# Feed-forward weight sums by adding transfers: turning the signs of a block scheme

## The chip, the core and the metric

The kernel runs on one core of a Trainium2 chip. Its five engines work in parallel and are tied by semaphores: TensorE (PE in the profile; PEld is its weight load), VectorE (DVE), ScalarE (ACT), GpSimd (POOL) and SyncE (SP). SP, and here also POOL, issue DMA transfers, which move data between the chip's main memory and the on-chip buffers. The metric is the device time in microseconds; the median of three runs is 1230.26 us (1228.70 to 1230.84).

## The reference, cut to what matters

Four decoder layers work on 256 tokens of width 1024. Layers 0 and 3 mix tokens with sparse attention (NSA), layer 1 with block attention (MoBA), layer 2 with a short gated convolution. After each mixer stands a dense feed-forward part with 2816 hidden columns:

```python
def swiglu(a, w_gate, w_up, w_down):
    return (jax.nn.silu(a @ w_gate) * (a @ w_up)) @ w_down

for i in range(DEPTH):
    a = rms_norm(h, norm_mix[i])
    h = h + mixer(a)                     # NSA, MoBA, convolution, NSA
    a = rms_norm(h, norm_ffn[i])
    h = h + swiglu(a, ffn_w_gate[i], ffn_w_up[i], ffn_w_down[i])
return rms_norm(h, norm_final)
```

Everything is float32. The change lies in `a @ w_gate` and `a @ w_up`.

## The kernel before

All weights stand in one array `w` of parts: a part is 128 x 1024 numbers (512 KB), eight tiles of 128 x 128, in the order in which PE uses them. A part is loaded by SP into one of six `raw` buffers (`load_part`), then split in two addends that the matrix engine multiplies: `whi`, a copy on ACT (L176), and `wlo`, the rest, a subtraction on DVE or, for a few named parts, on POOL (L180). Each product of float32 numbers is made of three matmuls: high by high, high by low, low by high. `whi` and `wlo` have five buffers each (`W_BUFS`), and `take` splits parts up to five ahead of their use (`AHEAD`), so ACT and DVE run ahead of PE until all five are full.

The feed-forward part (`ffn`) works through the hidden columns in groups of four tiles of gate and four of up: g = 0, 4, 8, 12, 16 and a last of two tiles. The groups 8 and 16 (`FAST_GROUPS`) go through `fast`: for the first four of the eight 128-row tiles of the inner dimension, tokens and weights are taken as 2 x 2 blocks, and seven block products take the place of eight. The weight blocks are B11, B12 (gate and up, first two tiles) and B21, B22 (gate and up, next two). Seven operands, in the order of `FAST`, are split into `shi` and `slo` (L136, L137) and multiplied (L442 to L444): B11, T1, B21, T2, B22, T4, T3. The T are sums and differences of blocks, which `combine` makes on DVE (L122):

```python
if what == "B11":
    b["T1"] = self.combine(b["B11"], b["B12"], b["B11"])   # B12 - B11
    b["T3"] = self.combine(b["B12"], b["B22"], b["B12"])   # B22 - B12
elif what == "T1":
    b["T2"] = self.combine(b["T1"], b["B22"], b["T1"])     # B22 - T1
elif what == "B21":
    b["T4"] = self.combine(b["B21"], b["B21"], b["T2"])    # B21 - T2
```

The four blocks are loaded by SP into four buffers of the tag `kx` (L132; `KX_BUFS`), which the `keys` of the two attention mixers also use. The sums on the token side are made by `token_sums` on POOL. The last four inner tiles of a fast group are ordinary parts, and their products (L476 to L478) are added to the same banks.

The hidden values are transposed on DVE, moved between partitions by 16 small transfers on SP (`move`, L411), and split into `ff` (`split`) at a set distance after the last move (`SPLIT_AFTER`, in half parts). `out_proj` multiplies them by the down weights (L226, L230).

Nobody writes the order of instructions on an engine out by hand: a scheduler takes the program in the order in which it is written, and puts each instruction on its engine's queue where its own estimate of times has its operands and buffers ready. On the chip each queue then runs strictly in that order: an instruction that waits holds everything behind it on its engine, and this holds for DMA issues on SP and POOL too. That is how loads of the feed-forward part's blocks come to stand amid the mixer ahead of it, where `kx` buffers come free of `keys`. POOL works in the attention mixers on the softmax scalings (L626) and on `wlo` of some output weights (L180).

Of the kernel before, what the change touches and what calls it, by code (L numbers as in the profile page):

```python
# [9 lines left out]
F32 = mybir.dt.float32  # L10
F32R = mybir.dt.float32r
AF = mybir.ActivationFunctionType
OP = mybir.AluOpType
# [10 lines left out]
DH = 64  # L24
# [9 lines left out]
MOVES = 4  # L34
SPLIT_AFTER = 4
FF_BUFS = 26
# [5 lines left out]
MOBA_ORDER = ("V k k q q k s V s T q q k s s P k T k q T P q P T P s q q T k s k T s s T P P T P P").split()  # L42
LO = {"nsa_out": "p", "moba_out": "vp", "A": "p", "F": "v"}
HI = {"moba_out": "v", "moba_q": "ava"}
# [4 lines left out]
FAST = ("B11", "T1", "B21", "T2", "B22", "T4", "T3")  # L49
FAST_GROUPS = (8, 16)  # L50
FFN_BANKS = ("BB BA", "AA AB", "BBAA", "AA BA", "BBAA", "B A")
KX_BUFS = 4
RUN = 2 * PART
LAG = 4
PROJ_BANKS = "AABB"
NSA_BY = ["p"] * 8
# [8 lines left out]
class Kernel:  # L65
    def __init__(self, ctx, tc, ap):
# [7 lines left out]
        self.raw = {}  # L74
        self.parts = {}
        self.jobs = []
        self.latest = []
# [42 lines left out]

    def combine(self, out, a, b):
        self.nc.vector.tensor_tensor(out=out, in0=a, in1=b, op=OP.subtract)  # L122
        return out

    def fast_part(self, x):

        q, what = self.seq[x]
        if what == "B11":
            self.blocks = {}
            for i, n in enumerate(("B11", "B12", "B22", "B21")):  # L130
                t = self.blocks[n] = self.block(n)
                self.load = self.nc.sync.dma_start(t, self.ap["w"][q + i])  # L132
        b = self.blocks
        hi = self.operands.tile([P, PART * P], F32R, tag="whi", name=f"shi{x}", bufs=W_BUFS)
        lo = self.operands.tile([P, PART * P], F32R, tag="wlo", name=f"slo{x}", bufs=W_BUFS)
        self.latest = [self.nc.scalar.copy(hi, b[what]),  # L136
                       self.nc.vector.tensor_tensor(out=lo, in0=b[what], in1=hi.bitcast(F32), op=OP.subtract)]  # L137
        self.parts[x] = (hi, lo)
        if what == "B11":
            b["T1"] = self.combine(b["B11"], b["B12"], b["B11"])  # L140
            b["T3"] = self.combine(b["B12"], b["B22"], b["B12"])
        elif what == "T1":
            b["T2"] = self.combine(b["T1"], b["B22"], b["T1"])
        elif what == "B21":
            b["T4"] = self.combine(b["B21"], b["B21"], b["T2"])

    def split_part(self, x):
        nc = self.nc
        q, what = self.seq[x]
        if what:  # L150
            self.fast_part(x)
            return
        lo_eng, hi_eng = (e.get(self.names[q], d) for e, d in ((LO, "v"), (HI, "a")))
        lo_eng, hi_eng = (e[q % len(e)] if q >= 4 else d for e, d in ((lo_eng, "v"), (hi_eng, "a")))
# [222 lines left out]
    def ffn(self, norm):  # L377
# [5 lines left out]
        q = P // 4  # L383
# [49 lines left out]
        def fast(tags):  # L433
# [45 lines left out]
            turned = self.sb([P, NT, 512], "pt", bufs=PT_BUFS)  # L479
            for t, (pg, eg), (pu, eu) in ((0, (gate0, p1), (up0, u2)), (1, (gate1, u3), (up1, p5))):  # L480
                nc.vector.scalar_tensor_tensor(eg, pg, r[t], eg, op0=OP.mult, op1=OP.add)
                nc.scalar.activation(eg, eg, AF.Silu)
                nc.vector.scalar_tensor_tensor(eu, pu, r[t], eu, op0=OP.mult, op1=OP.add)
                nc.vector.tensor_tensor(out=eu, in0=eu, in1=eg, op=OP.mult)
                nc.vector.transpose(turned[:, t], eu)
# [28 lines left out]
    def token_sums(self, norm):  # L514
# [7 lines left out]
        out = []  # L522
        for f, l, r, op in ((raw[0], a[1][0], a[1][1], OP.add), (raw[1], raw[0], a[0][0], OP.subtract),
                            (raw[2], a[0][0], a[1][0], OP.subtract), (raw[3], a[0][1], raw[1], OP.subtract)):
            nc.gpsimd.tensor_tensor(out=f, in0=l, in1=r, op=op)
# [210 lines left out]
    def nsa(self, j, norm):  # L736
# [12 lines left out]
        for a in range(2):  # L749
            nc.gpsimd.tensor_copy(xs[a][:, :, :, 16], pos[:, a, None, 8:].to_broadcast([P, 4, 8]))  # L750

        def put_raw(a, gp):
            def put(p):
                f = self.scaled(p)
                for i in range(2):
                    src = f[i * DH:(i + 1) * DH].rearrange("p (c r i) -> p i r c", i=2, r=8)
                    dst = xs[a][:, 2 * gp + i, :, :16]
                    nc.vector.tensor_copy(dst[:DH], src[:, 0])
                    nc.scalar.copy(dst[DH:], src[:, 1])
                if gp:  # L760
                    windows(a)
            return put

        def windows(a):
            for hf in range(2):
                for r in range(0, 8, 4):
                    x = self.ff([P, 2, S]).rearrange("p i s -> p (i s)").rearrange("p (r i g c) -> p r i g c", r=4, i=2, g=4)
                    src = xs[a][:, :, r:r + 4, hf:hf + 16].rearrange("p g r c -> p r g c")
                    nc.scalar.copy(x[:, :, 0], src)
                    nc.vector.tensor_tensor(out=x[:, :, 1], in0=src, in1=x[:, :, 0].bitcast(F32), op=OP.subtract)  # L770
                    if hf == 0:
# [494 lines left out]
```

## Time and profile before

| | |
|---|---|
| median of 3 runs | 1230.26 us |
| lowest, highest | 1228.70, 1230.84 us |
| profiled execution | 1231.72 us |
| its span, first to last instruction | 1229.9 us |
| granted TensorE clock, mean | 0.996 |
| PE, DVE, ACT, POOL busy | 98%, 80%, 60%, 23% of the span |
| moved by DMA | 231.40 MB, 213.33 MB of it read from main memory |

The profile is of one execution. A busy share is the sum of the instructions' durations; PE's matmuls overlap, so that 0.39 us stand for a matmul that starts 0.23 us after the one before it. "Idle before" is the time that an engine stood still ahead of a group of instructions, with the event that ended most of it. The feed-forward parts of the four layers run, by the chain of waits, from about 155 to 334, 451 to 629, 720 to 898 and 1044 to 1225 us; the mixers lie between.

### The profile page before, as it was taken

The numbers are of one execution on the slowest core, as the hardware profiler recorded it, in microseconds if no ns is written. First come the engines' busy times: TensorE is split into PE (matmuls) and PEld (weight loads), VectorE is DVE, ScalarE is ACT, GpSimd is POOL, SyncE is SP. The second block draws the span as 40 slices with busy tenths as digits, with TensorE's granted clock in tenths as the row PEclk, the third lists the DMA queues.
The fourth block names the chain that finished last, engine by engine and source line by source line (L and its number), as shares of the span: only waits on it lengthen the run. The fifth ranks groups of instructions, "written<-read, shape, count | busy, mean of one in ns | idle before, by whom it ended". The sixth has DMA issues, their size and how long they took to land.

```text
span 1229.9 us, 19380 instructions
## 1 busy us (share of the span) xinstructions
PE 1202.0 (98%) x6628; PEld 1043.2 (85%) x6628; DVE 985.2 (80%) x1743; ACT 732.5 (60%) x1300; POOL 288.0 (23%) x406
## 2 busy tenths in 40 slices
PE   7999999999999999999999999999999989999997
PEld 7988888888899888888888888888899878888886
DVE  7989788886778797887769797896759897889753
ACT  6789656564456535764444555574457896566543
POOL 1068640000111542000113260000230786400000
PEclk9899999999999999999999999999999999999999
DMA  8673265657654545666765655565647632655670
GB/s 313 221 235 88 85 225 165 211 183 252 193 172 154 167 136 175 240 202 194 278 197 164 191 183 175 200 237 164 244 155 244 207 115 74 208 177 198 200 266 35
DMA packets 96451, 231.40 MB, mean 188 GB/s; under 512 B 18272, under 2 KB 43232, under 8 KB 96352
## 3 DMA queue, kind: packets, MB, share of 16 engines
q1 hardware_dynamic: 95920, 229.61, 57.1%
q8 instruction: 52, 0.85, 0.3%
q10 hardware_dynamic: 432, 0.56, 0.1%
q14 instruction: 47, 0.39, 0.1%
HBM read 213.33 MB, written 1.05 MB: 174 GB/s over the span
## 4 chain that ended last, share of the span: by engine, by line
PE 83%; ACT 6%; DVE 5%; issue 2%; DMA 2%; POOL 1%; SPq 0%; POOLq 0%; ACTq 0%; DVEq 0%
PE psA L226 13%; PE psA L230 7%; PE psA L504 5%; PE psA L502 5%; PE psA L503 5%; PE psB L502 4%; PE psB L504 4%; PE psB L503 4%; ACT pr L622 3%; PE psA L208 2%; PE psA L206 2%; PE psA L207 2%; PE psB L226 2%; DVE wlo L180 2%; PE psB L444 1%
## 5 line engine op out<-in xcount | busy, mean ns | idle before, releaser
L176 ACT CAST whi<-raw 128x1024 fp32r<-128x1024 f32 (+1 forms) x363 | 373.3, 1039 | 289.6 <-DMA raw<-in_w 55.8
L180 DVE TENSOR_TENSOR wlo<-raw,whi 128x1024 fp32r<-128x1024 f32 (+1 forms) x350 | 428.3, 1241 | 130.1 <-ACT whi L176 106.4
L226 PE MATMUL psA<-ff,whi 128*128 128x512 f32 x686 | 181.8, 392 | 0.2 <-DVE row L1059 0.2
L226 PEld LDWEIGHTS psA<-ff,whi 128*128 128x128 f32 x686 | 124.8, 189 | 22.8 <-DVE row L1059 0.6
L626 POOL TENSOR_SCALAR pr<-pr,rc,gates 128x256 f32<-128x256 f32 (+1 forms) x128 | 76.9, 614 | 111.3 <-DVE rc L624 109.4
L206 PE MATMUL psA<-at,whi 128*128 128x256 f32 x352 | 101.3, 288 | 0.6 <-ACT whi L176 0.3
L208 PE MATMUL psA<-at,wlo 128*128 128x256 f32 x352 | 100.5, 286 | 1.1 <-DVE wlo L180 1.1
L230 PE MATMUL psA<-ff,wlo 128*128 128x256 f32 x686 | 101.0, 283 | 0.0
L230 PEld LDWEIGHTS psA<-ff,wlo 128*128 128x128 f32 x686 | 96.0, 191 | 5.3
L207 PE MATMUL psA<-at,whi 128*128 128x256 f32 x352 | 100.3, 285 | 0.0
L504 PE MATMUL psA<-whi,at 128*128 128x512 f32 x256 | 99.7, 389 | 0.0
L502 PE MATMUL psA<-whi,at 128*128 128x512 f32 x256 | 99.6, 389 | 0.0
L503 PE MATMUL psA<-wlo,at 128*128 128x512 f32 x256 | 99.6, 389 | 0.0
L136 ACT CAST shi<-B 128x1024 fp32r<-128x1024 f32 x56 | 58.9, 1051 | 54.2 <-DVE B L122 21.0
L293 POOL TENSOR_TENSOR ssq<-ssq,row 128x256 f32<-128x256 f32 x42 | 36.3, 864 | 207.9 <-ACT row L291 150.7
L180 POOL TENSOR_TENSOR wlo<-raw,whi 128x256 fp32r<-128x256 f32 x96 | 70.4, 767 | 34.7 <-issue 17.4
L137 DVE TENSOR_TENSOR slo<-B,shi 128x1024 fp32r<-128x1024 f32 x56 | 66.7, 1216 | 12.0 <-ACT shi L136 12.0
L502 PE MATMUL psB<-whi,at 128*128 128x512 f32 x192 | 75.2, 392 | 0.0
L504 PE MATMUL psB<-whi,at 128*128 128x512 f32 x192 | 74.8, 390 | 0.0
L503 PE MATMUL psB<-wlo,at 128*128 128x512 f32 x192 | 74.7, 389 | 0.0
L622 ACT ACTIVATE pr<-pr,mn 128x128 f32<-128x128 f32 (+1 forms) x160 | 71.2, 448 | 2.4 <-DVE mn L619 1.7
L206 PEld LDWEIGHTS psA<-at,whi 128*128 128x128 f32 x352 | 68.0, 193 | 1.9 <-DVE row L589 0.7
(293 smaller groups left out, 2688.4 us busy)
## 6 DMA issues: line engine op xcount, KB each, us to landing
raw<-in_w SPq DMA_DIRECT2D x368, 512.0 KB, 4.5
B<-in_w SPq DMA_DIRECT2D x32, 512.0 KB, 4.4
pt<-pt SPq DMA_DIRECT2D x320, 32.0 KB, 1.9
ff<-row SPq DMA_DIRECT2D x32, 64.0 KB, 3.4
keys<-keys SPq DMA_DIRECT2D x16, 128.0 KB, 2.9
h<-in_xt SPq DMA_DIRECT2D x4, 256.0 KB, 4.4
raw<-in_w SPq DMA_DIRECT2D x4, 256.0 KB, 4.7
pt<-pt SPq DMA_DIRECT2D x64, 16.0 KB, 3.1
```

The lines of the kernel that those rows point to most:

```text
L176: copy(hi[:, c], src[:, c])
L180: eng.tensor_tensor(out=lo[:, d], in0=src[:, d], in1=hi[:, d].bitcast(F32), op=OP.subtract)
L206: mm(out, wt[0], act[0], start=first, stop=False)
L207: mm(out, wt[0], act[1], start=False, stop=False)
L208: mm(out, wt[1], act[0], start=False, stop=last)
L226: mm(outs[o], w[0], acts[k].rearrange("p i s -> p (i s)"), start=(k == 0), stop=(k == n - 1))
L230: mm(outs[o][:, :S], w[1], acts[k][:, 0, :], start=False, stop=False)
L502: mm(o, a[:, 0, s], hi, start=(k == 0), stop=False)
L503: mm(o, a[:, 0, s], lo, start=False, stop=False)
L504: mm(o, a[:, 1, s], hi, start=False, stop=(k == KT - 1))
L622: nc.scalar.activation(pr[:, c], pr[:, c], AF.Exp, bias=mn[:, j:j + 1], scale=-1.0, accum_out=den[:, j:j + 1])
L626: {"p": nc.gpsimd, "v": nc.vector}[by[j % len(by)]].tensor_scalar(pr[:, c], pr[:, c], rc[:, j:j + 1], gates[j], op0=OP.mult, op1=OP.mult)
```

## The change

In place of four loads and four differences on DVE, a fast group now has:

- `start_sums`: SP loads B11 into a `kx` buffer t1 and B12 into t3; POOL then issues two transfers that add B12 to t1 and B22 to t3 as they write (`accum_op`). So T1 = B11 + B12 and T3 = B12 + B22. It is called up to 12 operands ahead of B11's split (`SUM_AHEAD`).
- B11 is loaded again, as an ordinary part, into a `raw` buffer; B21 and B22 are loaded into `kx` buffers when T1 is split. In all seven transfers of 512 KB a group where there were four: five by SP, two by POOL.
- T2 = T1 + B22 and T4 = T2 + B21 are still made on DVE, in place in t1.
- The signs of the token sums and of the last steps of `fast` are turned to match: subtractions for additions and the reverse, the same instructions on the same engines.
- `SPLIT_AFTER` goes from 4 to 6.

Three tables (`PAIRS`, `WINDOWS`, the entry `F` of `LO`) are new or longer, and name the same engine at each place as the code did before.

```diff
-SPLIT_AFTER = 4
+SPLIT_AFTER = 6
...
+SUM_AHEAD = 12
...
-    def combine(self, out, a, b):
-        self.nc.vector.tensor_tensor(out=out, in0=a, in1=b, op=OP.subtract)
-        return out
+    def start_sums(self, q):
+        nc, ap = self.nc, self.ap["w"]
+        self.blocks[q] = t1, t3 = [self.block(n) for n in ("T1", "T3")]
+        for t, i in ((t1, 0), (t3, 1)):
+            nc.sync.dma_start(t, ap[q + i])
+            nc.gpsimd.dma_start(t, ap[q + i + 1], accum_op=OP.add)
 
     def fast_part(self, x):
 
+        nc = self.nc
         q, what = self.seq[x]
-        if what == "B11":
-            self.blocks = {}
-            for i, n in enumerate(("B11", "B12", "B22", "B21")):
-                t = self.blocks[n] = self.block(n)
-                self.load = self.nc.sync.dma_start(t, self.ap["w"][q + i])
-        b = self.blocks
+        t1, t3 = self.blocks[q]
+        raw = {"B11": 0, "B22": 2, "B21": 3}
+
+        def load(name):
+            n = q + raw[name]
+            if n not in self.raw:
+                if name == "B11":
+                    self.load_part(n)
+                else:
+                    t = self.raw[n] = self.block(name)
+                    self.load = nc.sync.dma_start(t, self.ap["w"][n])
+            return self.raw[n]
+
+        if what == "T1":
+            load("B21")
+            load("B22")
+
+        def add(name):
+            nc.vector.tensor_tensor(out=t1, in0=t1, in1=load(name), op=OP.add)
+        if what == "T2":
+            add("B22")
+        elif what == "T4":
+            add("B21")
+        src = load(what) if what in raw else t3 if what == "T3" else t1
         hi = self.operands.tile([P, PART * P], F32R, tag="whi", name=f"shi{x}", bufs=W_BUFS)
         lo = self.operands.tile([P, PART * P], F32R, tag="wlo", name=f"slo{x}", bufs=W_BUFS)
-        self.latest = [self.nc.scalar.copy(hi, b[what]),
-                       self.nc.vector.tensor_tensor(out=lo, in0=b[what], in1=hi.bitcast(F32), op=OP.subtract)]
+        self.latest = [nc.scalar.copy(hi, src),
+                       nc.vector.tensor_tensor(out=lo, in0=src, in1=hi.bitcast(F32), op=OP.subtract)]
         self.parts[x] = (hi, lo)
-        if what == "B11":
-            b["T1"] = self.combine(b["B11"], b["B12"], b["B11"])
-            b["T3"] = self.combine(b["B12"], b["B22"], b["B12"])
-        elif what == "T1":
-            b["T2"] = self.combine(b["T1"], b["B22"], b["T1"])
-        elif what == "B21":
-            b["T4"] = self.combine(b["B21"], b["B21"], b["T2"])
 
     def split_part(self, x):
         nc = self.nc
+        for y in range(x, min(x + SUM_AHEAD, len(self.seq))):
+            q, what = self.seq[y]
+            if what == "B11" and q not in self.blocks:
+                self.start_sums(q)
...
-            for t, (pg, eg), (pu, eu) in ((0, (gate0, p1), (up0, u2)), (1, (gate1, u3), (up1, p5))):
-                nc.vector.scalar_tensor_tensor(eg, pg, r[t], eg, op0=OP.mult, op1=OP.add)
+            for t, (pg, eg), (pu, eu), op in ((0, (gate0, p1), (up0, u2), OP.add),
+                                              (1, (gate1, u3), (up1, p5), OP.subtract)):
+                nc.vector.scalar_tensor_tensor(eg, pg, r[t], eg, op0=OP.mult, op1=op)
...
-        for f, l, r, op in ((raw[0], a[1][0], a[1][1], OP.add), (raw[1], raw[0], a[0][0], OP.subtract),
-                            (raw[2], a[0][0], a[1][0], OP.subtract), (raw[3], a[0][1], raw[1], OP.subtract)):
+        for f, l, r, op in ((raw[0], a[1][1], a[1][0], OP.subtract), (raw[1], raw[0], a[0][0], OP.subtract),
+                            (raw[2], a[0][0], a[1][0], OP.add), (raw[3], a[0][1], raw[1], OP.add)):
```

How the scheduler's order moves is shown at three places. The first is DVE at the second fast group of layer 0, before; `slo` is the low part of an operand, and `B` a block or what was made of it:

```order
L180 TENSOR_TENSOR wlo_2876<-raw_2873,whi_2875 128x1024
L137 TENSOR_TENSOR slo_2904<-B_387_2895,shi_2903 128x1024
L122 TENSOR_TENSOR B_387_2895<-B_388_2897,B_387_2895 128x1024
L122 TENSOR_TENSOR B_388_2897<-B_389_2899,B_388_2897 128x1024
L137 TENSOR_TENSOR slo_2926<-B_387_2895,shi_2925 128x1024
L122 TENSOR_TENSOR B_387_2895<-B_389_2899,B_387_2895 128x1024
L137 TENSOR_TENSOR slo_2947<-B_390_2901,shi_2946 128x1024
L122 TENSOR_TENSOR B_390_2901<-B_390_2901,B_387_2895 128x1024
L137 TENSOR_TENSOR slo_2968<-B_387_2895,shi_2967 128x1024
```

The same place of the change, up to the split of the second sum; `T` is t1:

```order
L204 TENSOR_TENSOR wlo_2876<-raw_2873,whi_2875 128x1024
L163 TENSOR_TENSOR slo_2906<-raw_2903,shi_2905 128x1024
L163 TENSOR_TENSOR slo_2930<-T_376_2659,shi_2929 128x1024
L154 TENSOR_TENSOR T_376_2659<-T_376_2659,B_390_2927 128x1024
L163 TENSOR_TENSOR slo_2950<-B_389_2925,shi_2949 128x1024
L163 TENSOR_TENSOR slo_2971<-T_376_2659,shi_2970 128x1024
```

Two of four sums are gone there, and one of the two that are left comes later in the group, ahead of the split of T4. Further on in the group, two ordinary `wlo` now stand ahead of the four `ff` of an earlier group, where they stood behind them; the `ff` of the last group keep their place among the `wlo` of the down projection. The second place is POOL toward the end of MoBA in layer 1, before; `pr` are softmax weights that PE transposes next, `wlo` low parts of output weights:

```order
L626 TENSOR_SCALAR pr_4742<-pr_4742,rc_4745 128x256 x2
L180 TENSOR_TENSOR wlo_4852<-raw_4849,whi_4851 128x256 x4
L626 TENSOR_SCALAR pr_4896<-pr_4896,rc_4899 128x128 x2
L626 TENSOR_SCALAR pr_4896<-pr_4896,rc_4899 128x256 x2
L180 TENSOR_TENSOR wlo_5097<-raw_5094,whi_5096 128x256 x4
L626 TENSOR_SCALAR pr_4972<-pr_4972,rc_4975 128x128 x2
```

The same rows of the change; `T_643` is t1 and `T_644` t3 of the layer's first fast group:

```order
L651 TENSOR_SCALAR pr_4746<-pr_4746,rc_4749 128x256 x2
L130 DMA T_643_5394<-in_w 128x1024
L204 TENSOR_TENSOR wlo_4856<-raw_4853,whi_4855 128x256 x4
L651 TENSOR_SCALAR pr_4900<-pr_4900,rc_4903 128x128 x2
L651 TENSOR_SCALAR pr_4900<-pr_4900,rc_4903 128x256 x2
L130 DMA T_644_5395<-in_w 128x1024
L204 TENSOR_TENSOR wlo_5101<-raw_5098,whi_5100 128x256 x4
L651 TENSOR_SCALAR pr_4976<-pr_4976,rc_4979 128x128 x2
```

Each adding transfer is queued on POOL ahead of work of the mixer, and waits there for SP's load of the same buffer. NSA in layers 0 and 3 has the like: t1's between two `wlo`, t3's ahead of a softmax scaling. The third place is SP in layer 0's feed-forward part, around the loads for the second fast group, before:

```order
L132 DMA B_387_2895<-in_w 128x1024
L411 DMA pt_2600<-pt_2589 32x2x128 x8
L132 DMA B_388_2897<-in_w 128x1024
L132 DMA B_389_2899<-in_w 128x1024
L115 DMA raw_2747<-in_w 128x1024
```

The same place of the change, and the rows where the other two blocks now stand:

```order
L435 DMA pt_2601<-pt_2590 32x2x128 x3
L129 DMA T_376_2659<-in_w 128x1024
L129 DMA T_377_2660<-in_w 128x1024
L435 DMA pt_2601<-pt_2590 32x2x128 x5
L119 DMA raw_2755<-in_w 128x1024
...
L119 DMA raw_2903<-in_w 128x1024
L146 DMA B_389_2925<-in_w 128x1024
L435 DMA pt_2810<-pt_2799 32x2x128 x8
L146 DMA B_390_2927<-in_w 128x1024
L435 DMA pt_2810<-pt_2799 32x2x128 x8
```

The loads that the two adding transfers need stand where two blocks were loaded; the blocks B21 and B22 come later on SP, around the moves of the first fast group's hidden values.

More of the change, by code (lines that the diff above doesn't have):

```diff
@@ L42 @@
 MOBA_ORDER = ("V k k q q k s V s T q q k s s P k T k q T P q P T P s q q T k s k T s s T P P T P P").split()
-LO = {"nsa_out": "p", "moba_out": "vp", "A": "p", "F": "v"}
+LO = {"nsa_out": "p", "moba_out": "vp", "A": "p", "F": "vvvvvvvv"}
 HI = {"moba_out": "v", "moba_q": "ava"}
@@ L54 @@
 LAG = 4
+PAIRS = ("va", "va", "va", "va")
+WINDOWS = ("vvvv", "vvvv")
 PROJ_BANKS = "AABB"
@@ L75, in __init__ @@
         self.parts = {}
+        self.blocks = {}
         self.jobs = []
@@ L153, in split_part @@
         lo_eng, hi_eng = (e.get(self.names[q], d) for e, d in ((LO, "v"), (HI, "a")))
-        lo_eng, hi_eng = (e[q % len(e)] if q >= 4 else d for e, d in ((lo_eng, "v"), (hi_eng, "a")))
+        n = self.names[:q].count("F") if self.names[q] == "F" else q
+        lo_eng, hi_eng = (e[n % len(e)] if q >= 4 else d for e, d in ((lo_eng, "v"), (hi_eng, "a")))
         if lo_eng == "d":
@@ L479, in fast @@
             turned = self.sb([P, NT, 512], "pt", bufs=PT_BUFS)
-            for t, (pg, eg), (pu, eu) in ((0, (gate0, p1), (up0, u2)), (1, (gate1, u3), (up1, p5))):
-                nc.vector.scalar_tensor_tensor(eg, pg, r[t], eg, op0=OP.mult, op1=OP.add)
+            for t, (pg, eg), (pu, eu), op in ((0, (gate0, p1), (up0, u2), OP.add),
+                                              (1, (gate1, u3), (up1, p5), OP.subtract)):
+                nc.vector.scalar_tensor_tensor(eg, pg, r[t], eg, op0=OP.mult, op1=op)
                 nc.scalar.activation(eg, eg, AF.Silu)
-                nc.vector.scalar_tensor_tensor(eu, pu, r[t], eu, op0=OP.mult, op1=OP.add)
+                nc.vector.scalar_tensor_tensor(eu, pu, r[t], eu, op0=OP.mult, op1=OP.subtract)
                 nc.vector.tensor_tensor(out=eu, in0=eu, in1=eg, op=OP.mult)
@@ L750, in nsa @@
             nc.gpsimd.tensor_copy(xs[a][:, :, :, 16], pos[:, a, None, 8:].to_broadcast([P, 4, 8]))
+        copy_by = {"v": nc.vector.tensor_copy, "p": nc.gpsimd.tensor_copy, "a": nc.scalar.copy}
         def put_raw(a, gp):
@@ L757, in put @@
                     dst = xs[a][:, 2 * gp + i, :, :16]
-                    nc.vector.tensor_copy(dst[:DH], src[:, 0])
-                    nc.scalar.copy(dst[DH:], src[:, 1])
+                    for b, by in enumerate(PAIRS[2 * a + gp]):
+                        copy_by[by](dst[b * DH:(b + 1) * DH], src[:, b])
                 if gp:
@@ L764, in windows @@
         def windows(a):
+            lows = iter({"v": nc.vector, "p": nc.gpsimd}[by] for by in WINDOWS[a])
             for hf in range(2):
@@ L769, in windows @@
                     nc.scalar.copy(x[:, :, 0], src)
-                    nc.vector.tensor_tensor(out=x[:, :, 1], in0=src, in1=x[:, :, 0].bitcast(F32), op=OP.subtract)
+                    by = next(lows)
+                    by.tensor_tensor(out=x[:, :, 1], in0=src, in1=x[:, :, 0].bitcast(F32), op=OP.subtract)
                     if hf == 0:
```

## The prediction

> **What bounds the kernel now.** I read the page's first lines, then TensorE's waits, then stretches of the trace.
>
> ```profile
> span 1229.9 us, 19380 instructions
> PE 1202.0 (98%) x6628; PEld 1043.2 (85%) x6628; DVE 985.2 (80%) x1743; ACT 732.5 (60%) x1300; POOL 288.0 (23%) x406
> ```
>
> TensorE is busy all but 27.9 us of the span, so no change that leaves its matmuls alone can gain more than that. The question is where these microseconds lie. The view of waits, for TensorE (waits in total, times, longest), says:
>
> ```profile
> PE psA L254 <- ACT whi L176: 5.9, 1, 5.9
> PE psC L1016 <- DVE row L1028: 2.6, 2, 1.3
> PE psB L806 <- DVE row L589: 2.2, 2, 1.7
> ...
> PE psB L706 <- POOL pr L626: 0.7, 2, 0.5
> PE psB L704 <- POOL pr L626: 0.7, 1, 0.7
> ...
> PE psB L854 <- ACT row L844: 0.2, 1, 0.2
> ```
>
> L254 is the start of the kernel; the other lines belong to the mixers. No line of the fast groups (L442 to L444, L476 to L478) is among them. The groups by line say the same, with the idle time ahead of them as the last number, and the stretches of the gate and up products of the four layers show a TensorE that never stops (columns: length; busy of PE, PEld, DVE, ACT, POOL; clock; DMA share; GB/s):
>
> ```profile
> L442 PE MATMUL psB<-shi,ff 128*128 128x512 f32 x64 | 24.9, 389 | 0.0
> L443 PE MATMUL psB<-slo,ff 128*128 128x512 f32 x64 | 24.9, 389 | 0.0
> 156.90:272.80 115.90, 115.90 (x515) 96.02 (x514) 101.43 (x115) 70.00 (x92) 18.30 (x19) 1.00 0.61 200
> sum 463.90, PE 463.90 PEld 384.36 DVE 404.52 ACT 278.10 POOL 58.77; mean PE 115.97 PEld 96.09 DVE 101.13 ACT 69.52 POOL 14.69
> ```
>
> 463.90 us of TensorE in 463.90 us, at the full clock. VectorE is busy there 404.52 / 463.90 = 87%: close behind, but behind. So the reader is to see two places: feed-forward parts, where TensorE sets the pace and nothing waits, and mixers, where it sometimes waits for ACT, DVE and POOL.
>
> **What is removed.** The block sums on DVE and the block loads by SP:
>
> ```profile
> L122 DVE TENSOR_TENSOR B<-B,B x32: 1224/1225/1227, 191.1 to 1128.3; 128x1024 f32<-128x1024 f32 x32
> L132 SPq DMA_DIRECT2D B<-in_w x32: 327/377/530, 75.4 to 1106.2; - x32
> DMA to landing us min/median/max: 3.2/4.4/7.4
> ```
>
> Two of a group's four sums go: 16 x 1.225 = 19.6 us of DVE in all, 2.45 us a group. What it could be worth is read from the tightest spot, the change from the seven operands to the ordinary parts of a group:
>
> ```profile
> 201.99 3.46 DVE L137 TENSOR_TENSOR slo<-B,shi 128x1024 fp32r<-128x1024 f32 x3
> 206.70 2.39 DVE L180 TENSOR_TENSOR wlo<-raw,whi 128x1024 fp32r<-128x1024 f32 x2
> 208.95 0.39 PE L476 MATMUL psA<-whi,at 128*128 128x512 f32 x1
> 209.18 0.39 PE L477 MATMUL psA<-wlo,at 128*128 128x512 f32 x1
> ```
>
> The first ordinary `wlo` of the group is done at about 206.70 + 2.39 / 2 = 207.9 and TensorE takes it at 209.18 (L477): 1.3 us to spare. 2.45 us less DVE work, and two `wlo` put ahead of `ff` by the later `split`, widen this to about 4 us or more. TensorE did not wait before and does not after: **gain 0**. The turned signs are the same instructions; their cost is 0. The later `split` (two more half parts) takes work away from DVE's crowded spot; the `ff` of the last group keep their place in DVE's order among the `wlo` of the down projection, so nothing there gets later: 0.
>
> **What is added on SP and in DMA.** Eight more SP issues of 0.38 us, 3 us spread over eight groups, and three more transfers of 512 KB a group, 24 x 0.52 = 12.6 MB on 231. A fast group's TensorE time is 42 + 48 matmuls at 0.227 (209.18 - 208.95) = 20.4 us, so the DMA rate there rises by 1.6 MB / 20 us = 77 GB/s on some 200 at a share of 0.61: room is left. What could hurt is lateness. The tightest are second groups, whose loads start only when the first group frees its buffers. The before rows on SP, and TensorE's first two operands of the second group in layer 0:
>
> ```profile
> 207.30 1.00 SPq L132 DMA_DIRECT2D B<-in_w  x2
> 225.43 10.18 SPq L411 DMA_DIRECT2D pt<-pt  x16
> 241.59 0.39 PE L442 MATMUL psB<-shi,at 128*128 128x512 f32 x1
> 242.95 0.39 PE L442 MATMUL psB<-shi,ff 128*128 128x512 f32 x1
> 239.11 1.06 ACT L136 CAST shi<-B 128x1024 fp32r<-128x1024 f32 x1 [1.67 <-PE psA L504]
> ```
>
> T1's base is issued by about 207.3, where blocks were issued before, and lands 4.4 us later (7.4 at the most): 211.7 to 214.7. TensorE wants `shi` of T1 at 242.95 and `slo` 0.23 later, which the copy (1.06) and the subtraction (1.22) precede: the added sum must have landed by 240.9. That leaves 26 to 29 us for POOL's issue and the adding transfer. No row shows one; bounds are a plain load, 4.4, and several times that, as it also reads its target. I take 8.8, two loads' worth; even three times the worst, 22, fits: 0. B22 now stands on SP behind eight of the sixteen moves that begin at 225.43, so it goes out at about 225.43 + 10.18 / 2 = 230.5 and lands at 234 to 238. T2 needs it; before, ACT copied T2 only at 239.11, held by full buffers, and TensorE uses it at 241.59 + 3 x 1.36 = 245.7 (1.36 is the distance of two operands above). So 4 us or more of cover: 0. The raw loads behind the two T loads on SP shift by 2 to 3 us and have the five parts ahead to hide in.
>
> **What is added on POOL** is the only thing that reaches a mixer. Six of the sixteen adding transfers are queued there. Each holds POOL until its base has landed, and then for a time d, which no row shows: from below an issue by SP, 0.38; from above the whole landing, 4.4 (if POOL were held until the data is there). Nearest in kind is the issue, so I take d = 0.4. The rows of POOL and of the loads (the T now stand where these B stood), NSA of layer 0, then MoBA:
>
> ```profile
> 85.05 2.82 POOL L180 TENSOR_TENSOR wlo<-raw,whi 128x256 fp32r<-128x256 f32 x4 [0.99 <-ACT whi L176]
> 90.24 1.95 POOL L626 TENSOR_SCALAR pr<-pr,rc,gates 128x128 f32<-128x128 f32 x4 [2.37 <-DVE rc L624]
> 102.06 5.91 SPq L132 DMA_DIRECT2D B<-in_w  x2
> 106.10 4.39 POOL L626 TENSOR_SCALAR pr<-pr,rc,gates 128x128 f32<-128x128 f32 x8 [0.64 <-PE psB L998]
> 112.59 1.95 POOL L626 TENSOR_SCALAR pr<-pr,rc,gates 128x128 f32<-128x128 f32 x4 [2.10 <-DVE rc L624]
> ```
>
> ```profile
> 404.57 0.42 SPq L132 DMA_DIRECT2D B<-in_w  x1
> 410.74 3.01 POOL L180 TENSOR_TENSOR wlo<-raw,whi 128x256 fp32r<-128x256 f32 x4 [1.81 <-PE psB L707]
> 414.44 0.33 SPq L132 DMA_DIRECT2D B<-in_w  x1
> 418.11 2.03 POOL L626 TENSOR_SCALAR pr<-pr,rc 128x128 f32<-128x128 f32 x4 [4.36 <-DVE rc L624]
> 420.82 2.83 POOL L180 TENSOR_TENSOR wlo<-raw,whi 128x256 fp32r<-128x256 f32 x4 [0.69 <-PE psB L707]
> 424.69 1.62 POOL L626 TENSOR_SCALAR pr<-pr,rc 128x128 f32<-128x128 f32 x4 [1.04 <-DVE rc L624]
> ```
>
> NSA, t1: stands ahead of the `wlo` of 85.05; until the scaling at 90.24 POOL idles 0.99 + 2.37 = 3.36. t3: POOL comes free at 106.10 + 4.39 = 110.5, the base issued at 102.06 has landed by about 106.5; 2.10 idle before the scaling at 112.59. MoBA, t1: base landed at 404.57 + 4.4 = 409.0, as POOL comes free; some 6 us of idle time up to 418.11. t3: base landed at 418.8, POOL free at 418.11 + 2.03 = 420.1; 0.69 + 1.04 = 1.73 idle up to the scaling at 424.69, which transposes on TensorE wait for. Layer 3's NSA is taken as layer 0's. With every overrun passed on to TensorE:
>
> loss(d) = max(0, d - 1.73) + 2 max(0, d - 2.10) + 2 max(0, d - 3.36).
>
> d = 0.4 gives 0; d = 4.4 gives 2.7 + 4.6 + 2.1 = 9.4. The loss passes 2.5 us at d = 2.8. The ten other adding transfers stand where POOL has nothing due for tens of us.
>
> **The sum.** The profiled execution's 1231.72 us (span 1229.9 and 1.8 around it) minus 0 plus 0 stays 1231.72; it lies 1.46 over the median of 1230.26, which I carry over: **1230.3 us**. About 0.2%, 2.5 us, is what a measurement of this kernel can tell from no change.
>
> **Rivals.**
> 1. *POOL is held (slower).* An adding transfer keeps POOL far longer than an SP issue, and the softmax scalings queue up behind it, in MoBA first. It decides from d = 2.8 us. If POOL were held until the data lands, d = 4.4, the time is 1230.3 + 9.4 = 1239.7. If POOL could issue only while DVE idles, 13% of the time by the sum of the four stretches, 0.4 us would become 0.4 / 0.13 = 3.1: a loss of 1.4 + 2.0 = 3.4, 1233.7. For it: TensorE already waits for L626 (1.4 us above). Against it: issues on SP return in 0.38 us, long before the data lands, and POOL's and DVE's rows above run side by side. The Trainium skill, page "SBUF — State Buffer", section "SBUF: two separate sides", bears on the second form: a DMA issued from GpSimd waits for its descriptors while a DVE operation in a two-port mode holds the port that the two engines share, but a subtraction of two buffers, most of DVE's work here, blocks only GpSimd's reads. No run here shows a DMA issued by POOL, so the trace cannot yet say.
> 2. *The sums land late in second groups (slower).* If t1's sum lands after 240.9, TensorE stands at T1 in all four layers. A landing 2 us too late, 28 to 31 us after POOL's issue could begin, costs 4 x 2 = 8: 1238. Against it: that is four times the longest landing of the rows.
> 3. *DVE was closer to the path than shown (faster).* If spare DVE time carried into the mixer after a feed-forward part, the waits of NSA behind DVE could shrink: at the most L1016 and L806 in layer 3, half of 2.6 + 2.2, 2.4 us: 1227.9. Against it: DVE idles many times for TensorE and ACT between a fast group and the mixer, so a head start of 2.45 us is lost before.
>
> **How the numbers follow.** No change: 0.70. Rival 1: 0.15, rival 2: 0.05, both slower, 0.20 together. Rival 3, and unseen shifts of order that help: 0.10. The likeliest case lies within 2.5 us of 1230.3, about 1228 to 1232.7. The range takes in rival 3 and rival 1 up to d of about 3.4 (loss 1.7 + 2.6 + 0.1 = 4.4): 1227.5 to 1235.
>
> **What would show it.** Right: in the changed profile L122's successor (one in-place addition) counts 16 of 1.22 us, DVE's busy time is 19 to 20 us lower, TensorE's idle time ahead of the fast groups stays 0.0, its waits for POOL's `pr` stay near 1.4 us, reads rise to about 226 MB. Rival 1: POOL rows of the adding transfer, or idle ahead of the row behind, of 3 us and more, and larger waits `<- POOL pr`. Rival 2: waits of ACT or DVE for T, and of TensorE ahead of `shi` or `slo`. Rival 3: smaller waits at L806 and L1016 in layer 3. I am wrong if the median leaves 1227.8 to 1232.8.

## The result, and the profile after

The changed kernel takes 1240.96 us (median; 1238.77 to 1244.62), the kernel before, measured beside it, 1230.55. The ratio is 1.0083, with a 95% interval of 1.0067 to 1.0099: **slower by 0.8%, about 10 us**. Forecast were 1230.3 and no change, with a range up to 1235.0. The profiled execution took 1238.77 us, 7.05 more than that of the kernel before.

The page and the waits of TensorE in the changed kernel (waits in total, times, longest):

```profile
span 1236.8 us, 19444 instructions
PE 1204.6 (97%) x6628; PEld 1040.4 (84%) x6628; DVE 966.3 (78%) x1727; ACT 731.4 (59%) x1300; POOL 302.7 (24%) x422
```

```profile
PE psA L467 <- DVE slo L163: 2.4, 4, 0.8
...
PE psB L1027 <- POOL pr L651: 1.2, 2, 0.6
PE psB L731 <- POOL pr L651: 0.7, 2, 0.5
PE psB L729 <- POOL pr L651: 0.7, 1, 0.7
...
PE psB L1026 <- POOL pr L651: 0.4, 2, 0.2
...
PE psA L466 <- ACT shi L162: 0.2, 1, 0.2
```

VectorE lost its 18.9 us of work, and nothing came of it. Two kinds of wait are new. L466 and L467 are the products of the fast groups (L442 and L443 before), where TensorE had never stood; L1026 and L1027 are the transposes of the softmax in NSA, which wait for POOL's scalings (L651; L626 before). MoBA's waits for POOL, L729 and L731, are what they were.

To see how much stands where, I took from each trace the distance from every matmul's start to the next one's, less the usual distance of a matmul of that width (the 30th percentile), and summed the rest by place. TensorE's matmuls come in the same order in all kernels here, but for two neighbouring triples behind the seven products of a group that T4 delays, so places can be compared:

| us of TensorE, in one execution | before | after |
|---|---|---|
| seven block products, first fast groups (4 layers) | 0.0 | 0.96 (4 x 0.24) |
| seven block products, second fast groups | 0.0 | 4.47 (1.07, 0.54, 1.62, 1.24) |
| softmax of NSA, about 105 to 128 us, layer 0 | 4.51 | 5.66 |
| the same, layer 3 | 4.53 | 5.72 |
| one gap at the end of the second feed-forward part | 0.04 | 0.72 |
| all else | 24.9 | 23.0 |
| sum | 33.9 | 40.5 |

The first five rows grew by 8.5 us. All else fell by 1.9; but most of it is the other parts of the two NSA mixers, and there executions differ by that much among kernels whose mixers are the same (the layer-3 stretch ahead of its softmax took 5.6 to 8.1 us in the twelve kernels compared here). The profiled executions differ by 7 us and the medians by 10, so the table accounts for the 7. Three places are to be explained, and I show each once; the one gap of 0.7 follows at the end.

**The first groups: T4.** VectorE, ScalarE and TensorE of the changed kernel, first group of layer 0:

```profile
202.13 1.18 DVE L163 TENSOR_TENSOR slo<-B,shi 128x1024 fp32r<-128x1024 f32 x1
203.23 1.22 DVE L154 TENSOR_TENSOR T<-T,B 128x1024 f32<-128x1024 f32 x1
205.62 2.36 DVE L163 TENSOR_TENSOR slo<-T,shi 128x1024 fp32r<-128x1024 f32 x2 [1.17 <-ACT shi L162]
```

```profile
204.54 2.00 ACT L162 CAST shi<-T 128x1024 fp32r<-128x1024 f32 x2 [1.09 <-DVE T L154]
```

```profile
206.64 0.39 PE L466 MATMUL psA<-shi,at 128*128 128x512 f32 x1
206.90 0.50 PE L467 MATMUL psA<-slo,at 128*128 128x512 f32 x1
```

The same matmul in the kernel before:

```profile
206.46 0.39 PE L443 MATMUL psA<-slo,at 128*128 128x512 f32 x1
```

T4's addition now stands behind the split of B22, just ahead of its own split; before, it stood two operands earlier, behind that of B21, and T4's split was the second of the three that began at 201.99, done by about 204.3, some 2 us ahead of its use at 206.46. Addition, copy and subtraction follow each other: 203.23, 204.54, 205.62, done at about 206.8, and TensorE starts on `slo` at 206.90, 0.26 after the matmul before it and with a gap of 0.11 behind. 2.45 us of work less, and the operand is later than it was.

**The second groups: DMA is full, then everything is late.** The stretch from 210 to 220 us, before and after (length; busy of PE, PEld, DVE, ACT, POOL; clock; DMA share; GB/s), and what SP and POOL issued from 200 to 224 us, before and after:

```profile
210.00:220.00 10.00, 10.00 (x46) 8.28 (x45) 6.97 (x8) 5.90 (x10) 0.00 (x0) 1.00 0.87 291
```

```profile
raw<-in_w SPq DMA_DIRECT2D x7, 512.0 KB, 5.7
pt<-pt SPq DMA_DIRECT2D x16, 32.0 KB, 2.5
```

```profile
210.00:220.00 10.00, 10.00 (x46) 8.29 (x45) 8.18 (x11) 5.76 (x7) 0.89 (x1) 1.00 1.02 227
```

```profile
raw<-in_w SPq DMA_DIRECT2D x7, 512.0 KB, 7.4
T<-in_w POOLq DMA_DIRECT2D x2, 512.0 KB, 8.9
pt<-pt SPq DMA_DIRECT2D x16, 32.0 KB, 5.0
```

The engines of DMA are busy all the time and yet, as the profile counts bytes, move fewer than before (the share sums the packets' times, so it can pass 1). The two adding transfers of the second group (issued at 208.8 and 210.6) stand there beside the first group's moves and the raw loads behind them, and both land late. ScalarE's copy of the eighth ordinary part behind the sums, and the first group's last transpose on DVE, in the kernel before; and then what follows in the changed kernel on ACT, DVE, SP and PE:

```profile
217.45 1.05 ACT L176 CAST whi<-raw 128x1024 fp32r<-128x1024 f32 x1 [1.82 <-DMA raw<-in_w]
224.69 0.71 DVE L485 STREAM_TRANSPOSE pt<-ph 128x512 f32<-128x512 f32 x1
```

```profile
221.82 1.05 ACT L200 CAST whi<-raw 128x1024 fp32r<-128x1024 f32 x1 [5.51 <-DMA raw<-in_w]
```

```profile
228.95 0.70 DVE L510 STREAM_TRANSPOSE pt<-ph 128x512 f32<-128x512 f32 x1
239.30 1.22 DVE L154 TENSOR_TENSOR T<-T,B 128x1024 f32<-128x1024 f32 x1 [2.64 <-DMA B<-in_w]
248.89 1.23 DVE L163 TENSOR_TENSOR slo<-T,shi 128x1024 fp32r<-128x1024 f32 x1 [1.17 <-ACT shi L162]
```

```profile
229.68 5.08 SPq L435 DMA_DIRECT2D pt<-pt  x8
234.86 0.53 SPq L146 DMA_DIRECT2D B<-in_w  x1
```

```profile
250.17 0.50 PE L467 MATMUL psA<-slo,at 128*128 128x512 f32 x1 [0.71 <-DVE slo L163]
```

ScalarE waits 5.51 us for this raw part, where it waited 1.82. So the first group's last transpose is done 4.3 us later than before, so its moves begin at 229.68 where they began at 225.43, and B22, behind eight of them on SP, goes out at 234.86. VectorE stands 2.64 us with T2's addition until it has landed, and TensorE pays at T4, at the end of the same chain. "DVE T <- DMA B" stands in the waits of VectorE with 10.3 us in 4 places: one in each layer.

**NSA: the order on POOL.** POOL in the softmax of layer 0, SP's issue of T3's base, and a wait of TensorE there:

```profile
100.89 3.89 POOL L651 TENSOR_SCALAR pr<-pr,rc,gates 128x128 f32<-128x128 f32 x8
106.45 0.89 POOL L130 DMA_DIRECT2D T<-in_w  x1 [1.68 <-PE psA L1010]
107.10 4.28 POOL L651 TENSOR_SCALAR pr<-pr,rc,gates 128x128 f32<-128x128 f32 x8
```

```profile
101.37 0.38 SPq L129 DMA_DIRECT2D T<-in_w  x1
```

```profile
110.91 0.33 PE L1027 MATMUL psB<-ident,pr 128*128 128x128 f32 x1 [0.60 <-POOL pr L651]
```

T3's adding transfer stands ahead of the eight scalings that began at 106.10 before, 0.64 us after the batch ahead of them. I read its wait as one for its base, which SP issued 5.1 us earlier: by the trace the base landed at 105.90, and the transfers of the second groups begin 0.6 to 0.8 us behind the landing of their bases too (the profile names a matmul that had freed the buffer). The transfer takes 0.89 us itself, and the scalings start 2.3 us after the batch ahead of them is done, where it was 0.6.

### The profile page after: what moved, and what is told of

The parts are those of the page before. It is cut to its first block, busy times and chain, and to the rows that moved or that the text cites. A ratio compares the mean times of both kernels' runs of the same rounds, so it can differ in the third digit from the quotient of the medians.

```text
span 1236.8 us, 19444 instructions
## 1 busy us (share of the span) xinstructions
PE 1204.6 (97%) x6628; PEld 1040.4 (84%) x6628; DVE 966.3 (78%) x1727; ACT 731.4 (59%) x1300; POOL 302.7 (24%) x422
## 4 chain that ended last, share of the span: by engine, by line
PE 72%; DVE 9%; ACT 6%; DMA 5%; issue 3%; POOL 3%; SPq 2%; POOLq 0%; ACTq 0%; DVEq 0%
PE psA L250 11%; PE psA L254 6%; PE psA L527 4%; PE psA L529 4%; PE psA L528 4%; PE psB L527 3%; PE psB L529 3%; PE psB L528 3%; DMA raw<-in_w 3%; DVE wlo L204 2%; PE psA L232 2%; PE psA L230 2%; PE psA L231 2%; ACT pr L647 2%; PE psB L250 2%
## 5 line engine op out<-in xcount | busy, mean ns | idle before, releaser
L651 POOL TENSOR_SCALAR pr<-pr,rc,gates 128x256 f32<-128x256 f32 (+1 forms) x128 | 76.7, 646 | 107.3 <-DVE rc L649 106.7
L230 PEld LDWEIGHTS psA<-at,whi 128*128 128x128 f32 x352 | 67.6, 192 | 2.7 <-ACT whi L200 1.4
L232 PEld LDWEIGHTS psA<-at,wlo 128*128 128x128 f32 x352 | 67.5, 192 | 1.9 <-DVE wlo L204 1.9
L231 PEld LDWEIGHTS psA<-at,whi 128*128 128x128 f32 x352 | 67.7, 192 | 0.2
```

The source lines that it names most:

```text
L230: mm(out, wt[0], act[0], start=first, stop=False)
L231: mm(out, wt[0], act[1], start=False, stop=False)
L232: mm(out, wt[1], act[0], start=False, stop=last)
L651: {"p": nc.gpsimd, "v": nc.vector}[by[j % len(by)]].tensor_scalar(pr[:, c], pr[:, c], rc[:, j:j + 1], gates[j], op0=OP.mult, op1=OP.mult)
```

## The experiments

All changes are to the changed kernel, unless said otherwise. Two theories were there at first: **late block** (SP's order puts B22 behind moves) and **crowding** (the adding transfers fill the DMA engines); and, for both, the rival that the **mixers** cost it. What came out, with the places of the table above (us of TensorE in the profiled execution; "between" is from the first group to the second; NSA is the sum of the two softmax rows). The medians stand beside different runs of the kernel before (1230.41 to 1230.98), so the ratio is the surer column:

| kernel | median us | ratio to before, 95% | first | between | second | NSA |
|---|---|---|---|---|---|---|
| before | 1230.55 | | 0.0 | 0.0 | 0.0 | 9.0 |
| after | 1240.96 | 1.0067 to 1.0099 | 1.0 | 0.0 | 4.5 | 11.4 |
| signs and split alone | 1230.88 | 0.9996 to 1.0014 | 0.0 | 0.0 | 0.0 | 9.1 |
| adding in first groups only | 1235.17 | 1.0026 to 1.0050 | 1.2 | 0.0 | 0.0 | 11.5 |
| adding in second groups only | 1234.24 | 1.0026 to 1.0050 | 0.0 | 1.3 | 1.0 | 9.1 |
| blocks loaded early | 1245.99 | 1.0116 to 1.0143 | 1.0 | 7.9 | 0.9 | 11.4 |
| plain transfers for adding ones | 1234.49 | 1.0021 to 1.0045 | 0.9 | 0.0 | 1.2 | 10.7 |
| T4 early | 1236.90 | 1.0044 to 1.0068 | 0.0 | 2.5 | 0.0 | 11.7 |
| out of the mixers | 1239.04 | 1.0047 to 1.0071 | 1.0 | 0.0 | 4.7 | 9.1 |
| T3 later | 1234.32 | 1.0020 to 1.0042 | 0.9 | 0.0 | 1.7 | 9.1 |
| all mended | 1233.76 | 1.0009 to 1.0032 | 0.0 | 0.0 | 0.0 | 9.0 |
| first groups only, mended | 1232.26 | 0.9999 to 1.0023 | 0.0 | 0.0 | 0.0 | 9.3 |

### Signs and split alone

```diff
+    def by_dve(self, q):
...
+        return True
...
+    def dve_part(self, x):          # as before the change, with OP.add for the four sums
...
-            if what == "B11" and q not in self.blocks:
+            if what == "B11" and q not in self.blocks and not self.by_dve(q):
...
-            self.fast_part(x)
+            (self.dve_part if self.by_dve(q) else self.fast_part)(x)
```

> Turned signs and the later split as in the changed kernel, but all four sums of every group on VectorE and four plain block loads at B11, as before the change; no adding transfer at all. Theories 'late block' and 'crowding': 1230.5, within 0.2 percent of the kernel before. Rival 'signs or split': if turning the signs or the later split costs something, 1233 or more. Rival 'closer to the path': below 1228.

1230.88, ratio 1.0005. No cost or gain of the turned signs and the later split can be told.

### Adding transfers in one group of two

```diff
+    def by_dve(self, q):            # the second groups; the complement returns "not second"
+        second = q >= 2 * KT and self.names[q - 2 * KT] == "fast"
+        return second
...                                  # dve_part and the two conditions on by_dve as in the run before
```

> Adding transfers only in the first fast group of each layer (those whose adding transfers stand in POOL's queue in the mixers), the second group's four sums on VectorE with four plain loads. 'Late block' and 'crowding' put the loss into the second groups: 1231 to 1232, with 0.25 us of TensorE idle in each first group left. Rival 'mixers' (POOL's queue and the base loads in the mixers cost it): 1236 to 1240.

> The complement: adding transfers only in the second fast group of each layer, the first group's four sums on VectorE. 'Late block' and 'crowding': 1236 to 1240, with TensorE's waits for slo (L467 and L466 of the changed kernel) still there. Rival 'mixers': 1231 to 1232.

1235.17 and 1234.24: 4.8 and 3.8 us over the kernel before (1230.41 beside them), together 8.6 of the change's 10. Neither expectation held as written: the loss lies in both. With the first groups alone, NSA's 2.5 us and 4 x 0.24 us at T4 (and 0.27 more in one group) are there; with the second alone, 4 x 0.24 at T4 and, in one layer, 1.4 us between the groups. Alone, the second groups' transfers did not bring B22 too late. But here the scheduler's order changed as well: SP issues both block loads at 220.41, ahead of the sixteen moves that begin at 229.04, while the stretch from 210 to 220 us is nearly as crowded as in the changed kernel (share 0.92, 245 GB/s). With the first groups alone, the rival "mixers" was right for a part that the first comparison of the traces had hidden under the spread of the mixers.

### Blocks loaded early

```diff
             nc.gpsimd.dma_start(t, ap[q + i + 1], accum_op=OP.add)
+        for n, i in (("B21", 3), ("B22", 2)):
+            self.raw[q + i] = t = self.block(n)
+            self.load = nc.sync.dma_start(t, ap[q + i])
```

> The changed kernel, but the plain loads of blocks B21 and B22 are issued by SP directly behind the two bases of T1 and T3 instead of five parts ahead of their use. Theory 'late block': the changed kernel loses because B22 of a second group stands on SP behind eight moves, lands at about 239.3, and VectorE's addition for T2 and all that is behind it wait (DVE T <- DMA B 10.3 us in 4 places; TensorE L467 <- slo 2.4 us). Then this kernel has no DVE T <- DMA B wait, TensorE stands 4 to 5 us less in the second groups, and it takes about 1236 against 1241 of the changed kernel. Rival 'crowding': what is late is the whole of the DMA work from 208 to 226, which the adding transfers fill (share 1.02 from 210 to 220, 227 GB/s); two more loads in the same stretch make raw loads and moves later still, and the time stays at 1240 or more. Rival 'mixers': the time went in the mixers, 1241 as before.

1245.99: 5 us worse than the change itself. B22 is in time, and the second groups have their 4 x 0.24 alone. But the waits of TensorE now hold 6.8 us for the end of the first group's block (L509 is L506 in the changed kernel), because ScalarE waits still longer for a raw part (the one ahead of the eighth), and `gu` stands behind that part's `wlo` on VectorE:

```profile
PE psA L530 <- DVE gu L509: 6.8, 4, 2.5
```

```profile
221.58 1.05 ACT L203 CAST whi<-raw 128x1024 fp32r<-128x1024 f32 x1 [6.45 <-DMA raw<-in_w]
```

Two more loads in the full stretch move the loss to the next late one, and it grows. So "late block" alone is not the cause: it is how the crowding reaches TensorE. SP's order decides who pays and how much: 3.5 us in the second groups with B22 behind the moves, 7.9 between the groups in this run, and 1.3 and 2.5 where another change of order put both blocks behind the raw loads and ahead of the moves (second groups alone above, T4 early below).

### Plain transfers in place of adding ones

```diff
-            nc.gpsimd.dma_start(t, ap[q + i + 1], accum_op=OP.add)
+            nc.gpsimd.dma_start(t, ap[q + i + 1])
```

> The changed kernel, but the sixteen adding transfers are plain ones: same issue by POOL, same 512 KB, same wait for the base, but they overwrite T instead of adding to it (so the sums T1 and T3 are left out and the output is not the reference's). If the crowding comes from the adding, which reads its target too (a landing of 7.7 us against 4.5 of a plain load, the DMA share 0.99 at 200 to 290 GB/s), the raw loads behind it are on time again, the second groups' waits go, and what stays is 8 x 0.24 us at T4 and 2 x 1.2 us in NSA at the softmax scalings: about 1237. If what matters is the bytes or SP's order, or POOL's queue, it stays at 1240 to 1241.

This kernel leaves the addition out, so T1 and T3 are no sums and its output is not the reference's; it serves for the time alone. 1234.49, 6.5 us less than the change where about 4 were expected: the second groups' 3.5 us all but go, and NSA's loss falls from 2.4 to 1.7. POOL issues the same transfers in the same places, with the same bytes and the same waits for the base; what is gone is the adding (and 0.3 us of each issue). Rows of this kernel: the stretch from 210 to 220 us and VectorE's wait for B22; and the whole program's queue of POOL's transfers, first in the changed kernel, then in this one (packets, MB, share of 16 engines' span):

```profile
210.00:220.00 10.00, 10.00 (x46) 8.29 (x45) 7.85 (x10) 6.35 (x7) 0.53 (x1) 1.00 0.90 297
```

```profile
DVE T L154 <- DMA B<-in_w: 1.2, 1, 1.2
```

```profile
q0 software_dynamic: 2304, 8.39, 3.5%
```

```profile
q0 software_dynamic: 2304, 8.39, 2.0%
```

The share falls from 1.02 to 0.90 and the rate rises from 227 to 297 GB/s. An adding transfer holds the 16 engines 3.5% of 1236.8 us by 16, 2.7 us; the plain one 2.0% of 1233.1 by 16, 1.5 us. The bytes are counted once in both. The Trainium skill, page "Collectives: The Full Stack", section "The bandwidth ceiling: the fold count and why AG ≠ RS ≠ AR", says of ReduceScatter (a sum across cores) that its add in DMA needs two source reads on the same ring, and so moves at about half the rate (a factor of 1.93). The 1.75 here, for a kernel's own transfer, points the same way; no run here shows that the second read is what takes the time.

### T4 early

```diff
         if what == "T2":
             add("B22")
-        elif what == "T4":
-            add("B21")
-        src = load(what) if what in raw else t3 if what == "T3" else t1
+            t4 = self.raw[q + 3]                       # B21's buffer, already split
+            nc.vector.tensor_tensor(out=t4, in0=t4, in1=t1, op=OP.add)
+        src = load(what) if what in raw else {"T3": t3, "T4": self.raw.get(q + 3)}.get(what, t1)
```

> The changed kernel, but VectorE's addition for T4 goes into B21's buffer right behind the split of B21, where it stood before the change, instead of into T1's buffer at T4's turn. Theory: in each of the eight groups of the changed kernel TensorE stands 0.24 us at T4, because addition (1.22), copy (1.05) and subtraction (1.22) follow each other just ahead of its use. Then these 8 x 0.24 = 1.9 us go: 1239, with the first groups' TensorE idle time 0.0. The second groups' wait for B22 stays. If the T4 chain is not what TensorE waits for, 1241 and 0.24 us a group.

1236.90: 4 us less than the change where 2 were expected. The first groups' 4 x 0.24 are gone, as said. The second groups' waits went too, which was not expected; the reason stands on SP. The edit changed the scheduler's order, and both block loads now stand ahead of the moves:

```profile
221.27 0.91 SPq L146 DMA_DIRECT2D B<-in_w  x2
230.10 10.65 SPq L435 DMA_DIRECT2D pt<-pt  x16
```

The moves still begin late (230.10), so the crowding is there; in one layer it shows as 1.9 us of TensorE between the groups. This run therefore does not measure T4's share in the second groups by itself; the second groups alone, above, show it as 4 x 0.24.

### Out of the mixers, and T3 later

```diff
-            nc.sync.dma_start(t, ap[q + i])
-            nc.gpsimd.dma_start(t, ap[q + i + 1], accum_op=OP.add)
+            with self.tc.issue_after(self.load.ins):
+                nc.sync.dma_start(t, ap[q + i])
+                nc.gpsimd.dma_start(t, ap[q + i + 1], accum_op=OP.add)
```

> The changed kernel, but bases and adding transfers are ordered behind the latest weight load issued when their group is announced; this moves the first groups' adding transfers out of the mixers to the start of the feed-forward part, and leaves the second groups' where they were. Theory 'POOL order': in NSA the adding transfer of T3 stands ahead of eight softmax scalings and waits for its base to land (POOL idle 1.68, transfer 0.89), which costs TensorE about 1.2 us in each of two layers (waits for POOL pr at L1026 and L1027). Then these waits go, and the time is 1238 to 1239. Rival: the mixers do not matter and it stays at 1241.

```diff
+T3_AHEAD = 4
...                                     # start_sums now makes one pair a call, behind the latest weight load as above
-            if what == "B11" and q not in self.blocks:
+            if what == "B11" and (q not in self.blocks or y - x < T3_AHEAD and len(self.blocks[q]) < 2):
                 self.start_sums(q)      # first call: T1's pair of transfers, second: T3's
```

> As the run before (out of the mixers), and the base and adding transfer of T3 start some eight parts later than those of T1, so that in the second groups the two adding transfers no longer follow each other at 208.8 and 210.6. 'Crowding': the raw loads behind the first adding transfer come earlier, the second groups' TensorE waits fall from about 3.5 us (without the T4 share) by half or more: 1236 to 1237. Rival: the second adding transfer now collides with the next moves and loads, and the time is that of the run before or longer, 1239 or more.

Out of the mixers: 1239.04, 1.9 us less; the interval of its ratio overlaps that of the change a little. The trace is clearer: NSA's two stretches fall from 5.66 and 5.72 to 4.53 and 4.55, the values of before, and POOL's eight scalings start 0.60 us after the batch ahead of them, as they did before the change:

```profile
101.64 3.90 POOL L652 TENSOR_SCALAR pr<-pr,rc,gates 128x128 f32<-128x128 f32 x8
106.14 4.43 POOL L652 TENSOR_SCALAR pr<-pr,rc,gates 128x128 f32<-128x128 f32 x8 [0.60 <-PE psB L1028]
```

T3 later: 1234.32, 4.7 us less again; the second groups' 4.7 us fall to 1.7, of which 4 x 0.24 belong to T4. That is 3.0 of the 4.7; the rest of it has no place in the table. Nothing was removed: the same transfers start further apart, and B22 still stands behind eight moves (234.07). The DMA share from 210 to 220 us is 0.75. The eighth part, for which ScalarE waited 5.51 us, is there before ScalarE is free to copy it; the longest wait for a raw part is now 2.11, at the part ahead of it:

```profile
210.00:220.00 10.00, 10.00 (x45) 8.27 (x45) 8.07 (x11) 7.06 (x10) 0.00 (x0) 1.00 0.75 200
```

```profile
216.57 1.05 ACT L207 CAST whi<-raw 128x1024 fp32r<-128x1024 f32 x1 [2.11 <-DMA raw<-in_w]
218.22 1.05 ACT L207 CAST whi<-raw 128x1024 fp32r<-128x1024 f32 x1 [0.60 <-PE psA L509]
```

### All mended, and the first groups alone mended

> The changed kernel with three mends together: T4 added right behind the split of B21 (and B22's load, by that, ahead of the moves), bases and adding transfers out of the mixers, and T3's pair of transfers started later than T1's. If the three causes are separate, what they returned adds up: 1234.3 (the last two) less 8 x 0.24 = 1232.4, with TensorE's waits for slo and for the softmax scalings all but gone and the fast groups at 0.0 to 0.5 us. If the adding transfers cost something more that none of the three touches, 1234 stays.

> Adding transfers in the first fast groups only, out of the mixers, with T4 added early there; the second groups sum on VectorE from four plain loads. No cause that was found is left in it, and VectorE still makes 8 of the 16 sums less (9.8 us). If TensorE waits for VectorE nowhere in the feed-forward parts, as the prediction says, this is worth nothing: 1230.5, within 0.2 percent of the kernel before. If the saved sums were worth something behind the losses, 1228 or less; if adding transfers cost something that was not found, 1232 or more.

Both put the edits above together. With all three changes of order TensorE stands nowhere in the fast groups, nor between them, and NSA is at 9.0; the time is 1233.76, between the two expectations. By the ratio that is 2.5 us over the kernel before (1.1 to 3.9), and no place that the three causes touch holds it. In the profiled execution 0.8 us of it lie from the end of the first feed-forward part to the first fast group of the second, where the moved base loads now are (4.74 against 3.98); the rest is spread over the mixers within what executions differ. **What costs these last 2 us is open.**

With adding transfers in the first groups only, and mended, it is 1232.26, ratio 1.0011 (0.9999 to 1.0023): no change that can be told. VectorE's busy time there is 8.8 us lower than before, and that bought nothing. A hidden cost of some 1 us, for which the expectation set 1232 or more, is not excluded by this interval.

## Why the prediction was wrong

**What held.** TensorE sets the pace in the feed-forward parts, and VectorE's saved sums are worth nothing: the mended kernels have fewer sums, no wait in the fast groups, and are not faster. The signs and the split cost nothing that can be told (1.0005). The issue of an adding transfer did not hold POOL until the data was there: d was taken as 0.4 and is 0.89 (0.87 to 1.04), far from the 2.8 at which rival 1 was to decide, and MoBA's waits for POOL stayed at 1.4 us. No issue in the changed kernel took over 1.04 us with VectorE 78% busy, so the form of rival 1 that hung on the rule of the Trainium skill, page "SBUF — State Buffer", section "SBUF: two separate sides", did not occur here. T1's sum: 8.8 us were taken, the median landing is 7.7 and the longest 9.3:

```profile
T<-in_w SPq DMA_DIRECT2D x16, 512.0 KB, 4.5
T<-in_w POOLq DMA_DIRECT2D x16, 512.0 KB, 7.7
```

```profile
L130 POOL DMA_DIRECT2D T<-in_w x16: 867/887/1037, 83.3 to 1104.3; - x16
```

**What failed**, in the order of the prediction's steps:

1. *"2.45 us less DVE work, and two `wlo` put ahead of `ff` by the later `split`, widen this to about 4 us or more."* The step counted the sums removed and not the place of those kept. T4's addition moved from two operands ahead of its use to right ahead of it, and the 2 us that T4's low part had to spare became a gap of 0.24 in each of eight groups: 1.9 us. The 1.3 us of the prediction were read further on in the group, at the first ordinary part.
2. *"the DMA rate there rises by 1.6 MB / 20 us = 77 GB/s on some 200 at a share of 0.61: room is left."* A mean over a group. From 210 to 220 us the share was 0.87 before any transfer was added, and the added ones come in pairs right there. Nor is a byte that is added worth a byte that is copied: 2.7 us of the engines against 1.5. *"The raw loads behind the two T loads on SP shift by 2 to 3 us and have the five parts ahead to hide in"* hung on the same room: ScalarE's wait for one of them grew from 1.82 to 5.51 us.
3. *"so it goes out at about 225.43 + 10.18 / 2 = 230.5 and lands at 234 to 238 ... So 4 us or more of cover: 0."* The step took the time of the moves from the kernel before. They began 4.3 us later, for reason 2; B22 went out at 234.86 and VectorE got it at 239.30. With step 2 this cost about 3.5 us in the second groups (4.47 less their 4 x 0.24). Both were needed: with less crowding (plain transfers, T3 later) or with B22 ahead of the moves (second groups alone, T4 early) TensorE's wait in the second groups falls to T4's share or 0.8 us above it at most; with B22 ahead, though, 1.3 and 2.5 us stand between the groups instead.
4. *"t3: POOL comes free at 106.10 + 4.39 = 110.5, the base issued at 102.06 has landed by about 106.5; 2.10 idle before the scaling at 112.59."* The landing was right to 0.6 us (105.90). The place was wrong: the transfer stands ahead of the eight scalings of 106.10, where there was only 0.64 us of idle time. 1.15 and 1.19 us in the two NSA layers, 2.3 together. With d of 0.89 the formula of the prediction gave 0.

1.9 + 3.5 + 2.3 and 0.7 at the end of the second feed-forward part make 8.4 of some 10 us; about 2 stay open, as in the kernel with all three changes of order. At the 0.7, TensorE stands 0.41 us at 599.04 for the last `ff`, whose last moves SP issued at 592.18, where they went out at 584.79 before; the gap is 0.34 with the blocks loaded early, 0.65 with T4 early, and gone in all other runs, and no run was made for it. Rivals 1 and 2 named the right engine and the right groups with the wrong mechanism: not how long the transfer holds POOL but where it stands, and not T1's sum but T2's other operand. That rival 1's 1239.7 lies near the measured time is luck: by its own formula the d of this trace costs 0. Rival 3 did not occur.

## What to carry to other kernels

Where the engine that is relieved is not the one that is waited for, the saving is worth nothing and the side effects are all that is measured: look first for what moves, in each queue, and for the chain just ahead of each operand's use. Room in DMA is to be read in the 10 us in which the new transfers really run, not over a stage. A transfer that waits for another in an in-order queue belongs behind the work that the critical path needs next; where a scheduler places it, its place is to be looked up, not assumed. And an edit that goes through a scheduler can change more than it says: two of the runs here moved B22 ahead of the moves without being meant to.

## What was not expected of the hardware

An adding transfer of 512 KB, issued by POOL, lands in 7.7 us (median) where a plain one issued by SP takes 4.5 and a plain one issued by POOL takes 5.4, and it holds the DMA engines 1.75 times as long as a plain one. Its issue keeps POOL 0.89 us, that of a plain one 0.61:

```profile
T<-in_w POOLq DMA_DIRECT2D x16, 512.0 KB, 5.4
```

```profile
L130 POOL DMA_DIRECT2D T<-in_w x16: 527/613/785, 83.3 to 1102.2; - x16
```

From 200 to 224 us the small moves that SP issues land in 5.0 us (median) instead of 2.5, though they stand in another queue than POOL's transfers. Most of that is not the adding: with plain transfers in the same places it is 4.5. The Trainium skill, page "DMA: Bandwidth & Descriptors", section "Issuing engines are not separate DMA queues", says that transfers of all issuers run on the same 16 engines and interleave; the trace agrees.
